# New issue orders for out projection and FFN in a hybrid SSD and latent-attention layer

## The chip, the core and the metric

The kernel runs on one core of a Trainium2 chip. The metric is the device time of one execution in microseconds (us); smaller is better. Five engines of the core take part, each with an instruction stream of its own that it works off in order: TensorE (PE in the profile, with its weight loads listed apart as PEld), VectorE (DVE), ScalarE (ACT), GpSimd (POOL) and SyncE (SP). SP issues most of the transfers. Engines wait for one another through semaphores.

## What is computed

One layer of a streaming encoder for 512 prompt and 64 sample positions, with 1024 channels, in float32. The change lies in the last two parts:

```python
proj = rmsnorm(x, norm_mix) @ w_in
...
x = x + jnp.concatenate([y_ssd, o], axis=-1) @ p['w_out']
hf = rmsnorm(x, p['norm_ffn'])
x = x + (jax.nn.silu(hf @ p['w_gate']) * (hf @ p['w_up'])) @ p['w_down']
...
y = rmsnorm(x, norm_final)
```

`y_ssd` comes from a chunked state-space scan and `o` from latent attention over the same input. `w_gate` and `w_up` are 1024 x 2816, `w_down` is 2816 x 1024.

## The kernel before

**Layout.** Prompt and sample tokens stand side by side, 576 columns, and are worked on in halves of 288 (`TH`), so nearly every matmul is 128x288. Each float32 weight is split into a high part (a cast on ACT, L127) and a low part (a subtraction on DVE, L128), and each product is three matmuls: high by high, high by low, low by high. The names wh_... and wl_... are these two parts.

**Out projection** (L746 to L766). For eight tiles `t` of output channels and both halves, matmuls (L465) collect in a PSUM bank `ps_o`; then DVE adds the bank into `x` (L758). For some tiles ACT copies `x` into the bank first (L462) and the matmuls go onto it.

**FFN.** The gate and up products, and after them the down product, are made by a scheme of seven block products instead of eight. `gu_steps` (L949) shows what matters here:

```python
def m7():
    block_product(z, w, 7)
    act.copy(ur, z)
...
def m4():
    block_product(z, w, 4, onto=True)
    dve.tensor_tensor(ul, z, ul, ALU.add)
```

A product collects in a bank (`ps_x`, `ps_y` or `ps_z`), ACT or DVE reads the bank, and a later product is added onto what is still in it. So the first matmul of product 4 must come after ACT's copy, which must come after the last matmul of product 7: a round trip through PSUM. In `m1` ACT copies ps_x to ps_y (L959), in `m6` and `m7` the bank to `u` (L963, L967); `m2`, `m5`, `m4`, `m3` end in a DVE operation (L971, L975, L979, L983). `down_steps` (L1021) does the same with banks ps_dx, ps_dy and ps_dz; ACT copies go to `db` and `dc` (L1040), from where POOL adds them into `x` by a transfer (L1047), and DVE adds other banks into `x` (L1043, L1063, L1077). The last part of the down product goes through `ps_l` (L1104).

**Weights of the FFN** (`block_weights`, L841). Two SP transfers bring the weights of a block (`gu` or `db`): r2 first (L847), then r1 (L848). DVE makes four block sums: L850 reads r2 alone, L851 to L853 need r1 too. ACT casts part of r2 (`gu_a`, L855), DVE subtracts it for the low part (L861); the other operands go through L127 and L128. So before a matmul can use a low part wl_gu, DVE has made a sum, ACT has cast it and DVE has subtracted.

**What sets the order.** The program is written block by block, and a table then sets the order on each engine. `ISSUE` (L1315) has a text for each of the five engines that lists its instructions, by the numbers they got when they were made, in the order in which they are to be issued; `issue_in_order` (L1274) chains them. `PLACES` (L1286) says which buffer slot each tile gets.

```python
for name, text in ISSUE.items():
    made = [i for i in nc.cur_bb.bb.instructions if i.engine == engines[name].engine]
    order = list(_places(text))
    for a, b in zip(order, order[1:]):
        tc.add_manual_dep(made[b], made[a].name, info, reason="issue order")
```

Of the kernel before, what the change touches and what calls it, by code (L numbers as in the profile page):

```python
# [1328 lines left out]
1190-1192 1227 1193-1198 1291-1297 1199-1201 1228 1202-1204 1286-1288 1215-1217 1207-1210 1218-1220 1211-1214  # L1329
1221-1222 1298 1223 1299 1224 1318 1225-1226 1319 1301-1302 1300 1303-1317 1330-1332 1342-1343 1348-1350 1344-1346  # L1330
1351-1355 1347 1320-1326 1333-1335 1327-1329 1336-1341 1356-1363 1368-1370 1364-1367 1371-1378 1380-1388 1379
1389-1394 1404 1395-1397 1405 1398-1399 1406 1400-1402 1407-1408 1403 1409-1415 1428 1416-1427 1429-1433 1440-1441
1434 1572 1435 1442 1436-1437 1443 1438-1439 1444-1446 1584 1447 1452 1448 1453-1456 1449 1457-1458 1450 1459-1460
1578 1451 1461-1464 1579 1465-1472 1476 1587 1473-1474 1585 1475 1477-1481 1581 1482-1484 1575 1488 1485 1576
1486-1487 1489-1491 1588 1492-1495 1500-1501 1496-1497 1502 1498-1499 1503 1586 1504-1506 1573 1507-1510 1512-1514
1582 1605 1515 1511 1577 1516-1523 1574 1524 1593 1525 1580 1606 1526-1528 1536 1529 1583 1530 1589 1531 1537 1594
1532 1538 1533-1534 1595 1599 1608 1535 1539-1540 1600 1541 1607 1542 1601 1543-1546 1548 1547 1549 1626 1550 1602
1551-1555 1560-1563 1609 1564 1614-1615 1565 1610 1556-1557 1566-1567 1558 1568 1616 1620 1559 1627 1569-1571 1603
1635 1596-1597 1590 1598 1636 1617 1628 1621 1637 1604 1622 1629 1591 1623-1625 1592 1630-1631 1658 1647 1611 1641
1618 1612-1613 1659 1642 1660 1648 1644 1619 1661 1632 1638 1662 1643 1650 1633 1649 1663 1645 1664-1665 1634 1651  # L1340
1666 1656 1639 1653 1640 1652 1667-1668 1646 1669 1654-1655 1657 1694-1695 1670 1682 1671 1696-1697 1672-1675 1698
1676 1683 1699-1700 1677-1678 1718 1701 1679 1702 1719 1684-1685 1720-1721 1680 1703 1681 1686 1722 1704 1723 1687
1724 1688-1689 1725 1705 1690-1691 1706 1692 1707-1709 1693 1710-1711 1726-1728 1730-1732 1729 1733 1712-1716 1754
1734 1778 1717 1779 1735-1736 1755-1756 1780 1737 1757 1766 1738 1742-1744 1739 1745 1740 1758 1746-1747 1767 1748
1781 1741 1782 1759 1749-1750 1783 1751 1760 1752 1768 1761 1784 1769 1785 1770 1786 1753 1787 1771 1762 1772 1763
1802-1803 1788 1773 1789 1774 1804-1813 1764-1765 1775-1777 1862-1863 1838-1839 1864 1840-1841 1865-1866 1842
1867-1868 1843-1844 1869 1845-1848 1790 1870-1871 1814 1849 1791-1792 1872 1793 1873 1815 1794 1874 1795-1796 1816
1875-1876 1850 1877-1878 1797-1798 1817 1879 1818 1799 1819-1820 1880-1881 1821 1800 1882 1822 1801 1851-1855 1883
1823 1884 1824 1856 1826 1886 1827-1829 1825 1857 1830 1858 1831-1832 1859 1887 1885 1833-1835 1888-1889 1860 1890
1836 1861 1891-1893 1837 1894 1898-1900 1895-1897 1901 1910-1911 1902 1912 1946 1913 1903 1914 1904 1922-1924 1934  # L1350
1925-1926 1935 1905-1906 1936 1907 1915 1908 1916-1917 1937 1918-1921 1947-1948 1927 1938 1928 1949 1909 1950 1939
1970 1929-1930 1951 1931 1971 1940-1942 1932 1943 2024 1952 1933 1944 1953 1945 1954 2025 1955 1972 1956 1973 2026
1976 1958-1961 1977 1974 1957 1975 2027 1962-1965 2028 1978 1966-1969 2012 1979 2013 2029 1980-1981 1988 2014 2000
1982-1984 2001 1989-1991 2054 2048 1992 2055-2056 2042 1993 2043 1985-1986 2044 1987 2006 2015-2016 2057 1994 2002
2058 2003-2004 1995 2059 2005 2049 2017 2045 2007 2050 2046-2047 2008-2011 2051 2066 2018-2020 2030 2060 2067
2061-2062 2068 2021 1996 2022 2063-2064 2023 2069 2031-2032 2052 2065 2070 2036 1997 2037 2071-2072 2033 2084 2053
2034 2085 1998 2073 2038 2035 2086 2074-2075 1999 2078 2076 2087 2039-2040 2079-2080 2077 2088-2089 2081 2102 2041
2082 2090-2091 2103 2083 2092-2097 2104-2105 2098 2114 2099 2115 2100 2106 2138 2116-2117 2107-2109 2118 2101 2119
2110-2112 2120 2113 2126 2139 2127-2128 2192 2121 2129-2130 2144-2145 2131 2122 2140 2132-2133 2146-2147 2134-2135
2141 2148 2123-2124 2149 2136-2137 2142 2193 2125 2150 2143 2151 2194 2152 2195-2196 2153 2180 2156 2154 2197  # L1360
2157-2158 2168 2159-2162 2174 2163 2216 2222 2169 2181-2182 2155 2164 2170 2217 2175 2165-2166 2223 2171 2176-2177
# [12 lines left out]
2483-2484 2473 2485-2488 2516 2558 2492-2493 2461 2489 2494 2546 2517 2559 2518 2490 2519 2491 2495-2496 2504 2560
2520-2521 2505 2510 2497 2547 2506 2511 2548 2498-2499 2549 2500 2507 2550 2501 2552 2561 2502 2512 2508 2553 2562
2554 2513 2509 2555 2514-2515 2563 2570 2551 2522-2524 2556 2503 2525 2571 2557 2572 2564 2526 2565-2567 2527 2534
2573 2535 2568-2569 2582 2540 2574 2541 2575 2583 2588 2584 2536-2537 2585 2542-2543 2576 2586 2538-2539 2577 2589
2587 2578 2590 2544 2579-2581 2591 2606-2608 2545 2592 2609 2594 2593 2618 2610 2595 2611 2596-2597 2612 2598
2613-2615 2599 2619-2620 2600 2616 2601-2602 2621 2617 2603-2605 2622-2623 2642 2624-2625 2630-2631 2626 2632 2627
2648-2649 2643 2633 2628 2650 2634 2629 2635-2636 2696 2644 2637 2697 2645 2651-2653 2638-2641 2698-2699 2654-2655  # L1380
2700 2656 2660 2657 2646-2647 2661 2701 2662-2663 2720 2672-2673 2664 2674 2665 2684 2666-2667 2685 2668 2686 2714
2669 2675-2676 2678 2715 2726 2677 2687 2679 2688 2670 2680 2671 2681-2682 2716 2721 2690 2717 2727 2691 2658
2692-2693 2683 2738 2722 2694 2659 2718 2695 2702 2728 2703 2729 2689 2739 2730 2723 2719 2731 2724 2740 2704 2725
2732 2705 2733-2734 2708-2709 2735 2741 2706 2742 2707 2710 2736-2737 2743-2745 2750 2711 2756 2712 2746 2757 2747
2758 2748-2749 2751 2759 2752-2753 2774 2762-2763 2760 2754 2713 2764-2766 2761 2755 2767 2786-2788 2768-2770 2775
2789 2776-2780 2771 2790-2791 2772 2792-2793 2773 2794 2781-2782 2795 2783 2798-2800 2796 2784 2801 2810 2802-2804
2785 2805 2811 2797 2806-2807 2822 2812 2808 2813 2823-2824 2814 2809 2815 2825-2826 2816-2818 2827 2834-2835 2828
# [227 lines left out]
```

## Time and profile before

| what | value |
|---|---|
| time, median of 3 runs | 648.45 us (647.26 to 649.57) |
| profiled execution | 648.09 us, of which 646.0 us are the span |
| mean granted TensorE clock | 0.996 |
| out projection (L465, ps_o) | 159.3 to 257.7 us, with attention at first and FFN products at the end |
| first FFN block | from about 237 us, beside the out projection |
| FFN, gate, up and down | about 268 to 620 us |

A row of the timeline gives start, duration, engine, line, operation and `out<-in` by the program's names, with the shape and a count (x2 is two instructions merged into one row). What stands in brackets is the time that the engine stood idle just before, and who ended it. A row of a window table gives the stretch, its length, then busy time and instructions of PE, PEld, DVE, ACT and POOL, then granted TensorE clock, busy share of the DMA engines and GB/s. A matmul's end is modelled, and consecutive matmuls overlap in the rows; the distance from start to start is the one to read.

### The profile page before, as it was taken

The page shows a single profiled execution, that of the slowest core. Times are in us where ns is not written, and L with a number is a line of the kernel's source. Part 1 is how long each engine was busy: PE and PEld are TensorE (multiplying, and loading weights), DVE is VectorE, ACT ScalarE, POOL GpSimd, SP SyncE. Part 2 cuts the span into 40 slices and gives each one's busy share as a digit, 9 for nine tenths or more (in the row PEclk, how much of TensorE's full clock was granted, in tenths as well). Part 3 has the DMA queues.
Part 4 walks back from the last instruction along what each step waited for, and adds up shares of the span by engine and source line. Part 5 has one row for each costly group of instructions (what it writes and reads, how often), then busy time and mean ns, then how long its engine had stood idle before and what let it go on. Part 6 is the DMA issues. An engine that isn't in the chain of part 4 may idle for free.

```text
span 646.0 us, 11965 instructions
## 1 busy us (share of the span) xinstructions
PE 633.2 (98%) x4639; PEld 601.2 (93%) x4639; DVE 551.6 (85%) x980; ACT 389.6 (60%) x751; POOL 71.3 (11%) x111
## 2 busy tenths in 40 slices
PE   9999999999999999999999999999999999999994
PEld 9799999886787899999999999999999999999994
DVE  6999986899766599999998998789888889997764
ACT  7645425879766479855656565655564656545463
POOL 1422131101000000000012002100210011100022
PEclk9999999999999999999999999999999999999998
DMA  9521183313220221232185238432765166433004
GB/s 316 194 68 60 46 208 137 111 43 132 108 74 33 99 97 66 94 104 73 61 203 147 57 132 203 106 99 99 162 173 118 54 166 159 103 114 131 1 2 146
DMA packets 31560, 72.66 MB, mean 112 GB/s; under 512 B 3706, under 2 KB 11400, under 8 KB 31248
## 3 DMA queue, kind: packets, MB, share of 16 engines
q1 hardware_dynamic: 25360, 60.77, 28.9%
q0 software_dynamic: 5424, 10.57, 9.5%
q8 instruction: 36, 0.59, 0.4%
q10 hardware_dynamic: 720, 0.57, 0.3%
q14 instruction: 20, 0.16, 0.1%
HBM read 58.03 MB, written 3.30 MB: 95 GB/s over the span
## 4 chain that ended last, share of the span: by engine, by line
PE 81%; DVE 11%; DMA 2%; ACT 2%; issue 2%; POOL 0%; POOLq 0%; SPq 0%; DVEq 0%; ACTq 0%
PE ps_x L894 19%; PE ps_z L894 10%; PE ps_dx L1034 8%; PE ps_in L143 8%; PE ps_o L465 7%; PE ps_y L894 5%; PE ps_z L465 4%; PE ps_dz L1034 4%; PE ps_first L143 2%; PE ps_l L1104 2%; PE ps_dy L1034 2%; DMA gu<-in_w_gu 2%; PE sc L680 2%; PE pv L727 2%; PE ptp L702 1%
## 5 line engine op out<-in xcount | busy, mean ns | idle before, releaser
L894 PE MATMUL ps_x<-xop,wh_gu_S 128*128 128x288 f32 x504 | 126.4, 298 | 0.0
L894 PEld LDWEIGHTS ps_x<-xop,wh_gu_S 128*128 128x128 f32 x504 | 87.5, 188 | 1.3 <-DVE u L975 0.3
L894 PE MATMUL ps_x<-xop,wl_gu_S 128*128 128x288 f32 x252 | 73.1, 294 | 0.0
L894 PE MATMUL ps_z<-xop,gu_a 128*128 128x288 f32 x252 | 61.8, 298 | 0.0
L128 DVE TENSOR_TENSOR wl_gu_S<-gu,wh_gu_S 128x1024 fp32r<-128x1024 f32 x44 | 53.5, 1220 | 6.6 <-ACT wh_gu_S L127 6.0
L127 ACT CAST wh_gu_S<-gu 128x1024 fp32r<-128x1024 f32 x44 | 46.1, 1053 | 15.0 <-PE ps_y L894 6.3
L1047 POOL DMA_DIRECT2D x<-db x16 | 14.9, 943 | 296.7 <-ACT db L1040 152.5
L894 PEld LDWEIGHTS ps_x<-xop,wl_gu_S 128*128 128x128 f32 x252 | 47.0, 188 | 0.0
L894 PE MATMUL ps_y<-xop,wh_gu_A 128*128 128x288 f32 x168 | 45.5, 298 | 0.0
L143 PE MATMUL ps_in<-xs,wh_in 128*128 128x288 f32 x256 | 45.5, 298 | 0.0
L894 PEld LDWEIGHTS ps_z<-xop,gu_a 128*128 128x128 f32 x252 | 43.1, 188 | 0.6
L894 PE MATMUL ps_x<-xop,wh_gu_A 128*128 128x288 f32 x168 | 43.1, 297 | 0.0
L894 PE MATMUL ps_z<-xop,wh_gu_S 128*128 128x288 f32 x168 | 43.1, 296 | 0.0
L143 PEld LDWEIGHTS ps_in<-xs,wh_in 128*128 128x128 f32 x256 | 37.8, 189 | 0.2
L127 ACT CAST wh_gu_A<-gu 128x1024 fp32r<-128x1024 f32 x22 | 23.1, 1050 | 16.0 <-PE ps_x L894 6.7
L894 PEld LDWEIGHTS ps_y<-xop,wh_gu_A 128*128 128x128 f32 x168 | 30.2, 188 | 0.4
L894 PEld LDWEIGHTS ps_x<-xop,wh_gu_A 128*128 128x128 f32 x168 | 29.5, 188 | 0.2
L894 PEld LDWEIGHTS ps_z<-xop,wh_gu_S 128*128 128x128 f32 x168 | 29.5, 188 | 0.1
L465 PE MATMUL ps_o<-cat_y,wh_out 128*128 128x288 f32 x128 | 29.0, 313 | 0.5 <-DVE x L758 0.5
L128 DVE TENSOR_TENSOR wl_gu_A<-gu,wh_gu_A 128x1024 fp32r<-128x1024 f32 x22 | 26.8, 1218 | 2.8 <-PE ps_y L894 1.7
L465 PE MATMUL ps_o<-cat_o,wh_out 128*128 128x288 f32 x128 | 27.9, 300 | 0.2 <-DVE x L758 0.2
L143 PE MATMUL ps_in<-xs,wl_in 128*128 128x288 f32 x128 | 27.5, 296 | 0.0
(594 smaller groups left out, 2009.6 us busy)
## 6 DMA issues: line engine op xcount, KB each, us to landing
gu<-in_w_gu SPq DMA_DIRECT2D x44, 512.0 KB, 4.7
db<-in_w_down SPq DMA_DIRECT2D x16, 512.0 KB, 4.5
x<-db POOLq DMA_DIRECT2D x16, 288.0 KB, 4.4
x<-dc POOLq DMA_DIRECT2D x16, 288.0 KB, 4.3
wr_in<-in_w_in SPq DMA_DIRECT2D x8, 512.0 KB, 5.7
wr_out<-in_w_out SPq DMA_DIRECT2D x8, 512.0 KB, 3.2
cumb<-cumD SPq DMA_DIRECT2D x5, 512.0 KB, 4.5
x<-in_xT SPq DMA_DIRECT2D x2, 1152.0 KB, 5.8
```

The lines of the kernel that those rows point to most:

```text
L127: act.copy(hi, raw)
L128: dve.tensor_tensor(lo, raw, hi.bitcast(F32), ALU.subtract)
L143: pe.matmul(ps[:m, hf, :n], w, x[:, hf * n : (hf + 1) * n], start=start and k == 0 and i == 0, stop=stop and k == last and i == 2,)
L465: pe.matmul(ps[:, :n], w, x[:, cols], start=not onto and k == 0 and i == 0, stop=onto or (k == len(terms) - 1 and i == 2), skip_group_chec ...
L680: pe.matmul(s[:, :nk], qs[:, j, q0 : q0 + P], ks[:, j, :nk], start=True, stop=True)
L702: pe.transpose(pp[:, k : k + P], prs[p, i][:, j, b * P : b * P + P], ident)
L727: pe.matmul(pv[64 * j : 64 * j + 64, b * P :], V[b][:, h * HD : (h + 1) * HD], pts[p, b, j], start=b == 0, stop=True, skip_group_check=b > 0,)
L894: pe.matmul(ps, p, q, start=not onto and first and kp == kps[0] and j == 0, stop=onto or (last and kp == kps[-1] and j == 2), skip_group_c ...
L1034: pe.matmul(ps, l, r, start=not onto and k == 0 and j == 0, stop=onto or (k == n - 1 and j == 2), skip_group_check=onto,)
L1047: pool.dma_start(x2[t], v, accum_op=ALU.add)
L1104: pe.matmul(ps, w, x[:, cols], start=first and k == 0 and i == 0, stop=last and k == len(terms) - 1 and i == 2,)
```

## The change

Only rows of `ISSUE` are rewritten, from the out projection on. On PE 2632 matmuls stand at another place than before (moved by -50 to +56 places), on DVE 519 of 980 instructions (-22 to +38), on ACT 324 (-28 to +12), on SP 31 transfers (-2 to +3); POOL's order is the same. The instructions, their operands and the slots in `PLACES` are the same. Of the diff one piece is shown, the tail of SP's row; the others are of this kind:

```diff
     "SP": """
 11-14 16 15 18 17 19-20 22 21 25 24 39 23 37 26 40 33 38 41-43 34 44 32 45 81 46-48 57 64 79 59 58 56 62 61 65 63 60
-83 70 74 67 69 68 71 78 80 88 73 75 72 66 89 77 76 82 86 90-92 87 93 100 103 101-102 104-105 109-113 115 114 116-118
-120 119 121-122 124 123 125-128 130 129 131-132 134 133 135-136 138 137 139-140 142 141 143 145 144 146 148 147 150
-149 151-154 156 155 158 157 159-168 170 169 171-172 175-176 174 177-181
+83 70 74 67 69 68 71 78 80 88 73 75 72 66 89 77 76 82 86 90-92 87 93 100 103 101-102 104-105 109-118 120 119 122-123
+121 124-130 132 131 134 133 136 135 138 137 139-144 146 145 148 147 149-150 152 151 154 153 155-156 158 157 160 159
+161-169 171-172 170 175-176 174 177-181
```

What moves is better seen in the orders themselves, at three places. In the rows, numbers behind a name count the blocks (gu14 is the block of gate and up columns 14) and the buffers; x2 is two instructions in a row.

**PE, FFN block 14, about 488 us.** Product 7 ends with the matmul of xop3 by wl_gu14_S3 into ps_z14; product 4 begins with that of xop0 by gu14_a22. Before:

```order
L894 MATMUL ps_z14_5876<-xop3_3173,wh_gu14_S3_5867 128x288 x2
L894 MATMUL ps_x14_5874<-xop0_2937,wl_gu14_S1_5864 128x288
L894 MATMUL ps_z14_5876<-xop3_3173,wl_gu14_S3_5868 128x288
L894 MATMUL ps_x15_6001<-xop0_2937,wh_gu15_A11_5986 128x288
L894 MATMUL ps_x14_5874<-xop1_3026,wh_gu14_S1_5863 128x288 x2
L894 MATMUL ps_x14_5874<-xop1_3026,wl_gu14_S1_5864 128x288
L894 MATMUL ps_x14_5874<-xop2_3117,wh_gu14_S1_5863 128x288
L894 MATMUL ps_z14_5876<-xop0_2937,gu14_a22_5857 128x288 x2
```

and now:

```order
L894 MATMUL ps_z14_5876<-xop3_3173,wh_gu14_S3_5867 128x288 x2
L894 MATMUL ps_z14_5876<-xop3_3173,wl_gu14_S3_5868 128x288
L894 MATMUL ps_x14_5874<-xop1_3026,wh_gu14_S1_5863 128x288 x2
L894 MATMUL ps_x14_5874<-xop1_3026,wl_gu14_S1_5864 128x288
L894 MATMUL ps_x14_5874<-xop2_3117,wh_gu14_S1_5863 128x288 x2
L894 MATMUL ps_y14_5875<-xop3_3173,wh_gu14_A11_5859 128x288
L894 MATMUL ps_x15_6001<-xop0_2937,wh_gu15_A11_5986 128x288
L894 MATMUL ps_x14_5874<-xop2_3117,wl_gu14_S1_5864 128x288
L894 MATMUL ps_z14_5876<-xop0_2937,gu14_a22_5857 128x288 x3
```

Product 4 starts at the same place of PE's order; the last matmul of product 7 comes three places earlier, so nine places lie between the two starts instead of six.

**DVE, end of the out projection, about 223 to 228 us.** gu0 is the first FFN block, ps_o1_0_0 and ps_o1_0_1 are banks of the out projection that wait to be added into x. Before:

```order
L850 TENSOR_TENSOR gu0_2_2880<-gu0_0_2878 128x512
L852 TENSOR_TENSOR gu0_2_2880<-gu0_2_2880,gu0_1_2879 128x512
L758 TENSOR_TENSOR x2_0_2053<-ps_o1_0_0_2797,x2_0_2053 128x288
L853 TENSOR_TENSOR gu0_3_2881<-gu0_1_2879,gu0_2_2880 128x512
L861 TENSOR_TENSOR gu0_a22_2888<-gu0_0_2878,gu0_a22_2888 128x512
L851 TENSOR_TENSOR gu0_3_2881<-gu0_0_2878,gu0_1_2879 128x512
L758 TENSOR_TENSOR x2_0_2053<-ps_o1_0_1_2811,x2_0_2053 128x288
L128 TENSOR_TENSOR wl_gu0_A11_2891<-gu0_1_2879,wh_gu0_A11_2890 128x1024
```

and now:

```order
L850 TENSOR_TENSOR gu0_2_2880<-gu0_0_2878 128x512
L861 TENSOR_TENSOR gu0_a22_2888<-gu0_0_2878,gu0_a22_2888 128x512
L758 TENSOR_TENSOR x2_0_2053<-ps_o1_0_0_2797,x2_0_2053 128x288
L851 TENSOR_TENSOR gu0_3_2881<-gu0_0_2878,gu0_1_2879 128x512
L852 TENSOR_TENSOR gu0_2_2880<-gu0_2_2880,gu0_1_2879 128x512
L758 TENSOR_TENSOR x2_0_2053<-ps_o1_0_1_2811,x2_0_2053 128x288
L128 TENSOR_TENSOR wl_gu0_A11_2891<-gu0_1_2879,wh_gu0_A11_2890 128x1024
```

gu0_0 is r2, the first transfer, and gu0_1 is r1, the second. The first operation that reads r1 stood ahead of the sum into x of ps_o1_0_0 and now stands behind it; L861, which reads r2 and ACT's cast of it, stands there instead. On ACT that cast (L855, gu0_a22) has moved ahead of the cast of wh_gu0_A11, which reads r1.

**DVE, FFN block 18, about 548 to 552 us.** Before, from the split of S1 to that of S3:

```order
L128 TENSOR_TENSOR wl_gu18_S1_6663<-gu18_2_6648,wh_gu18_S1_6662 128x1024
L850 TENSOR_TENSOR gu19_2_6885<-gu19_0_6883 128x512
L1010 TENSOR_TENSOR pv17_1_6708<-u17_6412,pv17_1_6708 128x288
L852 TENSOR_TENSOR db16_None_2_6775<-db16_None_2_6775,db16_None_1_6774 128x512
L1063 TENSOR_TENSOR x2_1_2055<-ps_dy12_4_6522,x2_1_2055 128x288
L128 TENSOR_TENSOR wl_gu18_S3_6667<-gu18_3_6649,wh_gu18_S3_6666 128x1024
```

and now:

```order
L128 TENSOR_TENSOR wl_gu18_S1_6663<-gu18_2_6648,wh_gu18_S1_6662 128x1024
L852 TENSOR_TENSOR db16_None_2_6775<-db16_None_2_6775,db16_None_1_6774 128x512
L128 TENSOR_TENSOR wl_gu18_S3_6667<-gu18_3_6649,wh_gu18_S3_6666 128x1024
L1077 TENSOR_TENSOR x2_1_2055<-ps_dx12_4_6521,x2_1_2055 128x288
L1063 TENSOR_TENSOR x2_1_2055<-ps_dy12_4_6522,x2_1_2055 128x288
L1077 TENSOR_TENSOR x2_1_2055<-ps_dx12_6_6590,x2_1_2055 128x288
L1010 TENSOR_TENSOR pv17_1_6708<-u17_6412,pv17_1_6708 128x288
```

L850, L1010 and L1063 stood between the two splits; L1063 and L1010 now stand two and four rows behind the second one, L850 farther on.

More of the change, by code (lines that the diff above doesn't have):

```diff
@@ L1333 @@
[L1333 to L1337, printed above, removed]
@@ new lines @@
+1610 1617 1620 1623 1621 1635 1627 1622 1592 1636 1629 1637 1628 1611 1641 1618 1630 1624 1631 1612-1613 1625
+1658-1659 1642 1644 1650 1660 1647 1661-1662 1632-1633 1663 1651 1648 1664-1665 1619 1656 1638-1640 1666 1643 1667
+1634 1668 1645 1669 1646 1649 1652-1654 1657 1694 1670-1672 1695-1697 1673 1682 1698 1655 1674 1699 1675 1700 1718
+1683 1719 1676-1677 1701 1678 1684 1702 1679 1685 1703 1680 1704 1686 1681 1720 1687 1721 1688 1722-1723 1689 1724
+1690-1691 1706 1692-1693 1725 1707 1726 1705 1727-1728 1708-1709 1730 1710-1711 1729 1712 1731-1732 1713-1717
@@ new lines @@
+2484-2485 2460 2486 2461 2487 2492 2517 2493 2560 2518 2546 2504 2494 2488 2519 2552 2495-2497 2553 2505 2520 2547
+2506-2507 2521 2548 2498-2499 2549 2489 2500 2510 2501 2508 2502 2550-2551 2561 2490 2509 2554 2503 2511 2491 2555
+2512-2513 2562-2563 2514-2515 2570 2522-2523 2571 2524 2556 2525 2564 2526-2527 2557 2534-2535 2565 2572 2566-2569
+2540 2582-2584 2573 2541 2574 2542 2585 2575-2576 2536-2539 2588 2577 2589 2586 2578-2579 2590 2543 2580-2581
+2591-2592 2606-2609 2544 2610 2594-2595 2545 2593 2587 2596-2597 2611-2613 2598 2618 2599-2601 2619 2614 2602
@@ new lines @@
+2689 2707 2709 2745 2710 2746-2747 2711 2756 2748 2757 2749 2712 2750 2758 2751 2759-2760 2774 2752-2753 2762-2763
+2754 2775 2764-2765 2713 2766 2776 2761 2777 2786 2778 2755 2787 2767 2788-2790 2768 2791 2769 2779-2780 2792-2793
+2770 2794 2771-2773 2810 2795 2781 2796 2782-2785 2798-2800 2811 2801-2804 2812 2822 2805-2807 2813 2808-2809
+2823-2824 2814-2815 2825 2797 2826 2816-2817 2834-2835 2827-2828 2818-2820 2836 2821 2837 2829 2838-2839 2830 2840
+2858-2859 2846-2847 2870 2841 2860-2861 2871 2842-2844 2862 2848-2850 2863 2831-2832 2851 2845 2852 2864-2865
@@ new lines @@
+3354-3357 3398 3370 3358 3378 3399 3359-3360 3379-3382 3371 3337 3372 3361 3400-3401 3373 3383-3385 3402-3405
+3386-3389 3406 3390-3391 3410 3407 3392-3394 3408-3409 3411 3395-3397 3412-3416 3434 3417 3458 3418 3422 3419
+3423-3424 3435 3425 3420 3426-3428 3459 3446 3429 3436 3447 3430 3460 3431-3433 3437 3448 3438-3439 3421 3440 3449
+3441-3444 3450-3451 3445 3452 3461 3482 3453 3462 3454 3483 3463 3470 3455 3471-3472 3456 3464 3484 3536 3473 3465
+3474 3457 3537 3466 3475-3476 3485 3467 3486 3477 3487 3538 3478 3468 3539 3479 3488 3469 3480 3540 3481 3541 3489
@@ new lines @@
+3524 3490 3525 3491-3493 3512 3526 3494 3500 3554 3501 3495-3496 3513-3514 3497 3502-3503 3555-3556 3515 3504-3505
+3566 3516-3517 3567 3506-3509 3498 3527 3499 3560 3530 3518 3528-3529 3519 3561 3531 3557 3510 3520 3568 3562
+3521-3522 3511 3523 3532 3569 3558 3570 3533-3534 3559 3563-3564 3542 3578 3543 3535 3544 3579 3572 3565 3573
+3545-3546 3574 3580 3575 3581 3576-3577 3582 3547 3590 3583 3591 3548 3571 3584-3585 3592-3593 3549 3586-3588
+3550-3551 3589 3594 3614-3615 3552-3553 3595 3616 3596-3597 3617-3618 3598 3602 3619 3626-3627 3603 3628 3620 3599
@@ new lines @@
+3604-3605 3600-3601 3629 3621 3630 3622-3624 3606 3625 3607 3631 3608 3632 3609-3611 3633 3656 3634 3612-3613 3635
+3657-3660 3636 3661 3650 3638-3643 3651 3637 3644 3704 3645-3649 3652 3662-3663 3705-3706 3653-3654 3664 3668 3665
+3669 3666 3707 3655 3708 3670 3709 3667 3671-3675 3680 3676 3722 3677 3692 3678 3681-3683 3693-3694 3686 3684-3685
+3687-3689 3695 3679 3696 3723 3728 3698 3729 3699 3690 3724 3700 3725 3734-3735 3691 3726 3730 3727 3701-3702
+3736-3737 3703 3731-3732 3746 3733 3740 3710 3747 3711 3738 3741-3742 3716 3739 3758 3712 3759 3743 3697 3717
@@ L1445 @@
+4238 4170 4191 4198 4163 4192 4164 4193 4171-4172 4199 4165 4184 4200 4226 4173 4201 4174-4177 4239 4194 4227
+4207-4208 4228-4230 4240-4242 4202 4243 4231 4185 4209 4195 4262 4210 4186 4232 4211-4212 4263 4233 4213 4234 4214
+4235 4244 4264 4203 4215 4223 4217 4204 4220 4245 4236 4218 4237 4216 4265-4266 4219 4224 4246 4267 4221 4225
+4250-4251 4268-4270 4247 4271 4252 4274 4253 4275 4254 4276-4277 4248 4255 4222 4278-4279 4272 4256 4249 4273
+4257-4259 4280 4260-4261 4281-4391
 """,
@@ L1476 @@
[L1476 to L1478 removed]
+365 336 325 337 321 331 333 366 341 340 338 332 377 334 346 345 342 335 339 344 349 347-348 352 358 343 350-351 368
+353 359-360 356 354 361 355 357 369-373 376 374-375 382 389 378 383-384 379 386 390 385 380 387-388 381 405 397 393
@@ new lines @@
+825 831 834 824 832 860 853 835 842 836 850 859 849 843-844 851 847 845 861 846 838 837 848 852 854 862 839 863 881
+856 866 858 855 857 864-865 868 871 885 877 867 872 878 882 874 880 873 883 876 879 890 886 891 897 889 907 875 884
+888 903 909 887 910 898-899 904 911 900 892 901 919 906 915 908 912 893 914 913 869 905 920-921 923 870 922 917 894
+918 924-925 916 895 928 902 927 937 926 929 896 938 932 931 939 930 933-934 940 935-936 941 946 942 944 943 945 947
+951 949 948 954 950 952-953 955-979
@@ L1504 @@
+621 617-618 622 626 623 620 627-629 632 631 637 633-636 640 638-639 643 645 648 646 651 654 644 649 647 656 641 650
+657 655 659 658 663 660 642 661 664-665 652 666 662 674 667 669 653 675 670 668 677 676 671-672 686 673 684 680 678
+685 682 681 688-690 679 692 687 693-700 691 701-704 683 705-719
 """,
```

256 lines of the change are left out of this document (107 added, 149 removed).

## The prediction

> **What bounds the kernel now.** I read the busy shares and the chain of waits first, then two windows, then the timeline matmul by matmul.
>
> ```profile
> PE 633.2 (98%) x4639; PEld 601.2 (93%) x4639; DVE 551.6 (85%) x980; ACT 389.6 (60%) x751; POOL 71.3 (11%) x111
> PE 81%; DVE 11%; DMA 2%; ACT 2%; issue 2%; POOL 0%; POOLq 0%; SPq 0%; DVEq 0%; ACTq 0%
> 219.00:268.00 49.00, 48.14 (x348) 46.23 (x346) 45.07 (x78) 37.56 (x68) 0.00 (x0) 1.00 0.29 97
> 268.00:620.00 352.00, 350.98 (x2595) 346.71 (x2594) 309.74 (x494) 199.46 (x335) 28.65 (x33) 1.00 0.44 116
> 301.90 0.29 PE L894 MATMUL ps_z<-xop,wh_gu_S 128*128 128x288 f32 x1
> ...
> 303.62 0.29 PE L894 MATMUL ps_z<-xop,wl_gu_S 128*128 128x288 f32 x1
> ```
>
> TensorE is busy for 98% of the span and carries 81% of the chain. The change starts at about 200 us; from 268 to 620 us, the FFN, PE shows 350.98 of 352.00 us. That busy time hides something: a matmul's recorded 0.29 us overlaps the next one's. The pitch tells more. From 301.90 to 303.62 there are 13 intervals, so 0.132 us each. Giving each of the 2595 matmuls the median pitch of its own shape makes 344.3 us, so 7.7 us of the 352.00 is lost between matmuls; from 219 to 268 us the same count loses 3.6. No reordering can win more than these 11.3 us, as no matmul is taken away and the granted clock column already reads 1.00.
>
> Where the 7.7 us goes is seen at single matmuls:
>
> ```profile
> 488.33 0.29 PE L894 MATMUL ps_z<-xop,wl_gu_S 128*128 128x288 f32 x1
> 488.66 0.40 ACT L967 COPY u<-ps_z 128x288 f32<-128x288 f32 x1 [0.93 <-PE ps_z L894]
> ...
> 488.86 0.19 PEld L894 LDWEIGHTS ps_x<-xop,wh_gu_S 128*128 128x128 f32 x1
> ...
> 488.98 0.30 PE L894 MATMUL ps_x<-xop,wh_gu_S 128*128 128x288 f32 x1
> 489.11 0.30 PEld L894 LDWEIGHTS ps_z<-xop,gu_a 128*128 128x128 f32 x2
> 489.11 0.53 PE L894 MATMUL ps_z<-xop,gu_a 128*128 128x288 f32 x2
> 489.35 0.19 PEld L894 LDWEIGHTS ps_x<-xop,wh_gu_S 128*128 128x128 f32 x1
> 489.48 0.29 PE L894 MATMUL ps_x<-xop,wh_gu_S 128*128 128x288 f32 x1
> ```
>
> The matmul at 488.33 is the last of product 7 into ps_z. ACT copies that bank (488.66 to 489.06), and the matmul at 489.11 accumulates onto it. It comes exactly on the pitch (488.98 + 0.13), so it does not wait. Yet its weight load starts with it at 489.11, where an ordinary one starts 0.12 ahead (488.86 for 488.98). The next matmul then starts about 0.235 us later instead of 0.132: two matmuls take 489.11 to 489.48, 0.37 us, where two pitches are 0.26. So an operand that is ready 0.05 us before its use costs 0.10 us although nothing is shown as waiting.
>
> I paired every matmul from 268 to 620 us that waits for a VectorE or ScalarE result with the end of its writer: 334 of them. In 49 the writer ends less than 0.1 us ahead; in 39 by 0.1 to 0.2 (about 0.01 us lost each); in 246 by more, and these lose nothing. The first of the 49 and the last that stands clear in rows:
>
> ```profile
> 273.81 0.40 ACT L967 COPY u<-ps_z 128x288 f32<-128x288 f32 x1
> 274.27 0.65 PE L894 MATMUL ps_z<-xop,gu_a 128*128 128x288 f32 x3
> ...
> 605.49 0.46 DVE L975 TENSOR_TENSOR u<-ps_x,u 128x288 f32<-128x288 f32 x1 [1.55 <-ACT wh_dl L127]
> 606.00 0.52 PE L894 MATMUL ps_x<-xop,wh_gu_S 128*128 128x288 f32 x2
> ```
>
> Together the 49 lose 6.8 us: 2.09 in waits that show and 4.70 in late followers. Of them 37 are round trips through PSUM (matmul, copy or sum, matmul onto it): 0.50 + 3.52 = 4.0 us. Twelve are weight splits that end too late: 1.58 + 1.18 = 2.8 us.
>
> **The change part by part.** No instruction is added or removed; each slot stays. PE moves 2632 of its matmuls, DVE 519, ACT 324, SP 31, POOL none.
>
> *PSUM round trips, -3.6.* The trip of 489.11 needs 489.06 - 488.33 = 0.73 us plus some 0.05 to the next engine, 0.78; the old order gives it 6 places, 6 x 0.132 = 0.79. The new order puts the writer three rows earlier and leaves the user: 9 places, 1.19 us, a margin of 0.4. At 606.00 the distance goes from 6 to 14. Counted over all trips of one kind, the least distance rises from 6 to 9 for the copies of ps_x and ps_z to u, db and dc; to 9 for the sums into u; to 7 to 9 for the rest. Bounds: 0 if ScalarE is late for another reason, 4.0 if every one is cured. ScalarE has room (199.46 busy of 352.00), so I take nine tenths: -3.6.
>
> *Weight splits, -2.2.* The two large ones:
>
> ```profile
> 455.13 1.22 DVE L128 TENSOR_TENSOR wl_gu_A<-gu,wh_gu_A 128x1024 fp32r<-128x1024 f32 x1
> 456.40 0.40 PE L894 MATMUL ps_x<-xop,wl_gu_A 128*128 128x288 f32 x1 [0.43 <-DVE wl_gu_A L128]
> 551.71 1.22 DVE L128 TENSOR_TENSOR wl_gu_S<-gu,wh_gu_S 128x1024 fp32r<-128x1024 f32 x1
> 552.98 0.40 PE L894 MATMUL ps_z<-xop,wl_gu_S 128*128 128x288 f32 x1 [0.59 <-DVE wl_gu_S L128]
> ```
>
> The first loses 0.59 us against its pitch and its follower 0.1; the new order takes a 0.68 us sum (L850) out from ahead of the split and puts the matmul four places later (0.53). The second loses 0.75; its split now comes four VectorE places earlier, three short operations of 0.45 to 0.69 us being moved behind it, and its matmul two places later. Both are cured. The ten small ones hold the other 1.2 us; most get one to three places. From 0 to -2.8; I take -2.2.
>
> *Out projection, -1.2.*
>
> ```profile
> 224.01 0.29 PE L465 MATMUL ps_o<-cat_o,wl_out 128*128 128x288 f32 x1
> ...
> 224.72 0.69 DVE L852 TENSOR_TENSOR gu<-gu,gu 128x512 f32<-128x512 f32 x1 [1.17 <-DMA gu<-in_w_gu]
> 225.33 0.45 DVE L758 TENSOR_TENSOR x<-ps_o,x 128x288 f32<-128x288 f32 x1
> 224.73 1.05 ACT L127 CAST wh_gu_A<-gu 128x1024 fp32r<-128x1024 f32 x1 [4.52 <-DMA gu<-in_w_gu]
> 225.68 0.62 ACT L855 CAST gu_a<-gu 128x512 fp32r<-128x512 f32 x1
> ...
> 225.84 0.54 PE L465 MATMUL ps_o<-cat_y,wh_out 128*128 128x288 f32 x2 [0.48 <-DVE x L758]
> ```
>
> The bank's last matmul ended at 224.30, but its sum stood on VectorE behind L852, which waits for the second weight transfer. PE lost 0.64 us and its follower 0.10. In the new order L861 stands there, which needs the first transfer and ScalarE's cast of it; then x, and only then L851 and L852. ScalarE, idle for 4.52 us up to 224.73, now does that cast ahead of wh_gu_A instead of behind it. So x can run from 224.3, a wait of none: -0.74. The same wait at 238.32 (0.4 with its follower) shrinks by what is moved ahead of it. The losses at 233.39 and 253.33 keep their distances. From -0.5 to -2.0; I take -1.2. Had the cover gone, with x behind another late transfer, it would cost the same 0.64 again.
>
> *New waits, +1.6.* Giving margin to one operand takes it from another, on VectorE above all:
>
> ```profile
> 240.00:260.00 20.00, 19.96 (x148) 19.42 (x147) 19.66 (x36) 18.84 (x38) 0.00 (x0) 1.00 0.23 75
> 280.00:300.00 20.00, 20.00 (x148) 19.55 (x147) 19.87 (x33) 12.03 (x20) 0.00 (x0) 1.00 0.35 103
> 430.00:460.00 30.00, 29.57 (x221) 29.07 (x221) 28.29 (x46) 18.05 (x33) 1.83 (x3) 1.00 0.32 90
> ```
>
> There VectorE has no idle time to give. From 430 on the new order pushes two sums into x (0.45 us each) 38 and 22 places back into this stretch, its splits come one to three places later, and several matmuls come earlier. I count two operands late by up to 0.8 us there, and some six new close pairs elsewhere at 0.10 us plus a little. From 0 to one split each (1.22 + 0.10 = 1.3 us) on five places, 6.6; I take 1.0 + 0.6 = 1.6, near the rows of before, where that stretch lost 1.1 us in all.
>
> *SP's queue.* It issues the same weight loads; 31 move by at most three places. Where a load now stands in front of one whose slot is not free yet, the loads behind it wait. The first VectorE user of a load was mostly 2 to 3 us behind its landing, and the slots come free earlier by the same moves, so zero; one load would come about 1.2 us late, on a VectorE that is idle there. Without that slack it would cost those 1.2 us.
>
> Sum: -3.6 - 2.2 - 1.2 + 1.6 = -5.4. The profiled execution took 648.09 us, 646.0 of it span; it becomes 642.7 with a span of 640.6. Against the median of the runs, 648.45, it is 643.1.
>
> A rule stands against the main term. The Trainium skill, page "TensorE: Matmul & The Clock Gate", in its overview of the engine, says that PE's queue pulls weight loads ahead of matmuls in flight. By it the load behind the late matmul would be done in time, no 0.10 us would hang on a margin, and without the 4.70 us of followers the change would be worth what the first rival below gives. The trace agrees at ordinary matmuls (load at 488.86 for 488.98) but not at 489.11, whose load and whose follower's load (489.35) came late; I go by the rows.
>
> **The rivals.** *Only visible waits go.* If the late follower belongs to any matmul that carries a wait, whatever its margin, the 4.70 us stays. Then 2.09 us and the 1.2 of the out projection, less 1.6 of new waits, make -1.7: 646.8. (The page's rule would give this time too.) Or the waits are eaten further: 648. For it: the profile names no releaser for most of those 0.10 us. Against: 246 matmuls carry such waits with over 0.2 us to spare and keep the pitch. This holds too if the moves cure the places but the time comes back elsewhere.
>
> *Almost all is won.* All three gains at their far ends (4.0 + 2.8 + 2.0) and no new wait: -8.8, 639.7. For it: VectorE has 309.74 of 352.00 in use, so some 42 us of room. Against: that room isn't where it is needed.
>
> *VectorE falls behind.* In the stretches 240 to 330 and 428 to 450 us, where it is 94 to 99% busy, an operation that moves forward delays all splits behind it, with no idle time to catch up in, and PE waits once per split: 1.3 us each. The gains before new waits are 7.0 us, so it decides from six late splits (7.9); with seven, 9.2, the time is 650.7. For it: moves of 38 places into a full queue. Against: before, with the queue just as full, the losses there were 1.1 us from 430 to 460.
>
> **How the numbers follow.** Forecast (-3 to -8) 0.58; almost all 0.10; only visible waits or no net change 0.19; VectorE behind 0.13. The time is the forecast's, 643.1, with a range of its own from 640.5 to 645.5. The range over the cases goes from 640.0, which cuts off part of "almost all", to 648.8, which leaves out VectorE behind. About 0.3%, 1.95 us, is what a measurement of this kernel tells from no change. Faster by more: the forecast, almost all, and a quarter of the third case, 0.73. Within: most of the third, 0.15. Slower: 0.12.
>
> **What would show it.** Right: ACT's copy at what was 488.66 ends 0.3 us or more before its matmul, whose load starts 0.13 ahead and whose follower comes 0.13 later; 268 to 620 shrinks to about 347.5; fewer than 20 close pairs; no wait for x of L758 near 225. Wrong: PE waits for wl splits from 240 to 330 or 428 to 460 of over 3 us; or the close pairs are gone and the time is not, which would refute the 0.10 us.

## The result: 639.6 us, 8.7 us less

The changed kernel took 639.63 us (median of 4 runs, 639.24 to 640.2), the kernel before 648.32 beside it; the ratio is 0.9866 with an interval from 0.9847 to 0.9885. Four later series on other occasions gave 641.36, 639.72, 639.92 and 639.6 us, which is 6.4, 8.0, 7.8 and 8.2 us less than the kernel before beside them. The forecast was 643.1 us with a range from 640.0 to 648.8: the direction was right, and the gain was larger than the range allowed.

The page's first rows and its chain are read first; the profile of the changed kernel has

```profile
span 637.5 us, 11950 instructions
PE 626.2 (98%) x4639; PEld 598.0 (94%) x4639; DVE 551.4 (86%) x980; ACT 390.4 (61%) x751; POOL 70.7 (11%) x111
PE 48%; issue 1%; DVE 1%; ACT 1%; POOL 1%; POOLq 0%; DVEq 0%
```

PE is still busy for 98% of the span, so this share tells nothing of the gain: it counts the overlapping 0.29 us of each matmul, late followers included. The chain's shares add up to only about half of the span here, so its 48% cannot be held against the 81% before. What does tell is how long a like piece of the program takes. The windows of the kernel before, from the same place of PE's order (the 1695th matmul) to the last gate or up matmul:

```profile
270.45:610.70 340.25, 339.23 (x2514) 335.07 (x2512) 303.37 (x482) 193.60 (x326) 27.77 (x32) 1.00 0.45 120
```

and of the changed kernel, from one matmul farther on:

```profile
268.13:601.43 333.30, 333.20 (x2508) 332.26 (x2507) 303.30 (x483) 194.16 (x329) 27.75 (x32) 1.00 0.46 121
```

From the same matmul, which starts at 268.00 now, the FFN takes 6.8 us less with the same work on VectorE and ScalarE (303 and 194 us). Four matmuls, 0.6 us, have only moved behind the window's end; the rest, some 6 us, was lost time. By the count used in the prediction (each matmul at the median pitch of its shape) the FFN lost 7.66 us before and 1.93 now. That count hangs on the median: a tenth of a nanosecond in it makes 0.25 us over some 2500 matmuls, so half a microsecond between two profiles means nothing. Instead of 49 close pairs between 268 and 620 us there are 7.

The matmul of the prediction's example, which stood at 489.11:

```profile
481.94 0.29 PE L894 MATMUL ps_z<-xop,wl_gu_S 128*128 128x288 f32 x1
...
482.27 0.40 ACT L967 COPY u<-ps_z 128x288 f32<-128x288 f32 x1 [0.77 <-PE ps_z L894]
...
482.99 0.45 PEld L894 LDWEIGHTS ps_z<-xop,gu_a 128*128 128x128 f32 x3
...
483.12 0.56 PE L894 MATMUL ps_z<-xop,gu_a 128*128 128x288 f32 x3
483.38 0.32 PEld L894 LDWEIGHTS ps_x<-xop,wh_gu_S 128*128 128x128 f32 x2
483.51 0.43 PE L894 MATMUL ps_x<-xop,wh_gu_S 128*128 128x288 f32 x2
```

The trip takes what it took (481.94 to 482.67), but the user comes at 483.12, 0.45 us behind. Its weight load starts 0.13 us ahead, and three matmuls take 483.12 to 483.51, 0.39 us, the bare pitch.

The wait for x at 225.84 is gone too, as the rows of VectorE and PE show:

```profile
223.47 0.69 DVE L861 TENSOR_TENSOR gu_a<-gu,gu_a 128x512 fp32r<-128x512 f32 x1
224.08 0.45 DVE L758 TENSOR_TENSOR x<-ps_o,x 128x288 f32<-128x288 f32 x1
224.45 0.68 DVE L851 TENSOR_TENSOR gu<-gu,gu 128x512 f32<-128x512 f32 x1
224.87 0.43 PE L465 MATMUL ps_o<-cat_y,wh_out 128*128 128x288 f32 x2
```

In the stretch from the 1282nd matmul to the 1695th (out projection and first FFN block) 60.61 us became 58.02 in this profile. It is not always so: the four later profiles of the changed kernel show 59.2, 59.6, 58.0 and 59.3, and the experiments tell why.

### The profile page after: what moved, and what is told of

Read it like the earlier page. It is cut to its first block, busy times and chain, and to the rows that moved or that the text cites. A ratio compares the mean times of both kernels' runs of the same rounds, so it can differ in the third digit from the quotient of the medians.

```text
span 637.5 us, 11950 instructions
## 1 busy us (share of the span) xinstructions
PE 626.2 (98%) x4639; PEld 598.0 (94%) x4639; DVE 551.4 (86%) x980; ACT 390.4 (61%) x751; POOL 70.7 (11%) x111
## 4 chain that ended last, share of the span: by engine, by line
PE 48%; issue 1%; DVE 1%; ACT 1%; POOL 1%; POOLq 0%; DVEq 0%
PE ps_x L894 17%; PE ps_dx L1034 9%; PE ps_z L894 9%; PE ps_dz L1034 5%; PE ps_y L894 4%; PE ps_dy L1034 2%; PE ps_l L1104 2%; POOL x L1157 0%; DVE x L1145 0%; DVE sq_last L1194 0%; DVE ss L1192 0%; POOL ss L1238 0%; POOLq L1600 0%; ACT sq L1233 0%; ACT x L1149 0%
```

## The experiments

All kernels compute the same; only the order tables differ. Each edit is shown in short: what is taken from the old and the new tables, or the rows of one of the places that are moved. In the tables' words, "old" and "new" are the orders before and after the change.

### Which part of the program the gain comes from

At about 270 us old and new orders of each engine hold the same instructions ahead of a cut (1694 on PE, 456 on DVE, 343 on ACT, 78 on SP), so they can be joined there.

```diff
 e1_out
-PE, DVE, ACT, SP: old ahead of the cut, old behind
+PE, DVE, ACT, SP: new ahead of the cut, old behind
 e2_ffn
-PE, DVE, ACT, SP: old ahead of the cut, old behind
+PE, DVE, ACT, SP: old ahead of the cut, new behind
```

> New orders up to about 270 us on every engine, old orders behind. Margin theory: the losses between matmuls up to there fall by 2.3 us and the FFN keeps its close pairs, so about 646.0 us. If the stages depend on each other (the out projection's gain is only kept because the FFN's new order takes it up), less than 1 us is won.

> Old orders up to about 270 us, new orders behind. Margin theory: the FFN wins its 6.2 us by itself, about 642.1 us, and this and the other half add up to the whole gain of 8.7. If the FFN's gain needs the earlier start of transfers and sums in the out projection, clearly less than 6.

The new FFN behind the old out projection took 642.0 us against 648.12, ratio 0.9909 (0.9891 to 0.9927): 6.1 us less, as expected. The new out projection alone took 647.32, ratio 0.999 (0.998 to 1.0): of the 2.3 us that were expected hardly 0.8 are left. In its profile the stretch up to 270 us is shortened as expected (58.43 us), but the FFN behind it loses 9.04 us instead of 7.66. Some 0.6 us of that is lost at 268 to 274 us, by operands that are late now that PE comes 2 us earlier, and 0.8 us at one matmul (476.98), whose operand stands on VectorE behind a weight transfer that took 8.4 us instead of 7.6. VectorE and PE there:

```profile
474.30 0.69 DVE L850 TENSOR_TENSOR gu<-gu 128x512 f32<-128x512 f32 x1 [3.28 <-DMA gu<-in_w_gu]
...
476.98 0.40 PE L894 MATMUL ps_x<-xop,wh_gu_A 128*128 128x288 f32 x1 [0.63 <-DVE g L983]
```

So the second theory, that the out projection's gain is only kept because the FFN's new order leaves room for it, fits this profile, but it is not shown by the times: the series of the changed kernel that followed (e5_after) gained 6.4 us, no more than the two halves together.

In e2_ffn one wait is left that is worth a look. ACT, then PE:

```profile
350.57 0.40 ACT L963 COPY u<-ps_x 128x288 f32<-128x288 f32 x1 [3.74 <-DMA x<-db]
...
351.02 0.40 PE L894 MATMUL ps_x<-xop,wh_gu_S 128*128 128x288 f32 x1 [1.71 <-ACT u L963]
```

The copy writes a buffer that GpSimd's transfer of db into x still reads. It waits for a landing, and PE for the copy. The same pair is the one old close pair that the changed kernel did not open (347.68 in its profile, margin 0.05 us); its wait was 0 to 0.4 us in the five profiles of the changed kernel.

### Whether a margin is worth time

e4_open leaves all orders as they were and only brings matmuls of other banks ahead of the user of each close trip through PSUM. At the example:

```diff
 L894 MATMUL ps_x14_5874<-xop2_3117,wh_gu14_S1_5863 128x288
-L894 MATMUL ps_z14_5876<-xop0_2937,gu14_a22_5857 128x288 x2
 L894 MATMUL ps_x14_5874<-xop2_3117,wh_gu14_S1_5863 128x288
 L894 MATMUL ps_y14_5875<-xop3_3173,wl_gu14_A11_5860 128x288
+L894 MATMUL ps_z14_5876<-xop0_2937,gu14_a22_5857 128x288 x2
 L894 MATMUL ps_x14_5874<-xop2_3117,wl_gu14_S1_5864 128x288
```

> The old orders of all engines but PE; on PE two or three unrelated matmuls are brought ahead of the first matmul behind each of 35 of the 36 close round trips through PSUM in the FFN (162 places hold another matmul). Visible waits removed: 0.44 us; late followers removed: 3.31 us. Margin theory: 3.7 us less, about 644.6 us. Rival that only visible waits cost time: 0.4 us less, 647.9. Rival that the new orders win by what VectorE, ScalarE and the transfers do earlier: no change.

It took 645.41 us, ratio 0.9958 (0.9946 to 0.9971), 2.7 us less (3.0 in the span of the profile). The 0.4 us of visible waits cannot be that. What is missing to 3.7 went in part where PE now comes sooner to a split that is no sooner done. VectorE, then PE:

```profile
548.84 1.22 DVE L128 TENSOR_TENSOR wl_gu_S<-gu,wh_gu_S 128x1024 fp32r<-128x1024 f32 x1
...
550.11 0.40 PE L894 MATMUL ps_z<-xop,wl_gu_S 128*128 128x288 f32 x1 [0.82 <-DVE wl_gu_S L128]
```

This is the wait of 552.98, 0.75 us before and 0.98 now. A dozen places that lost nothing before lose 0.05 to 0.15 us each, while the wait of 456.40 shrinks from 0.59 to 0.19. In the whole FFN the close pairs fell from 48 to 23 and the loss from 7.66 to 4.57 us.

The opposite test takes margin away from the changed kernel: in each of 35 trips the first matmul behind the copy or sum goes two, three or four places forward, past matmuls of other banks. Three places, at the example:

```diff
 L894 MATMUL ps_x14_5874<-xop2_3117,wh_gu14_S1_5863 128x288 x2
+L894 MATMUL ps_z14_5876<-xop0_2937,gu14_a22_5857 128x288
 L894 MATMUL ps_y14_5875<-xop3_3173,wh_gu14_A11_5859 128x288
 L894 MATMUL ps_x15_6001<-xop0_2937,wh_gu15_A11_5986 128x288
 L894 MATMUL ps_x14_5874<-xop2_3117,wl_gu14_S1_5864 128x288
-L894 MATMUL ps_z14_5876<-xop0_2937,gu14_a22_5857 128x288 x3
+L894 MATMUL ps_z14_5876<-xop0_2937,gu14_a22_5857 128x288 x2
```

> The changed kernel again, as the base for the three that follow: 639.6 us.

> The changed kernel, with the first matmul behind each of 35 round trips through PSUM (margins 0.45 to 0.51 us) two places earlier on PE, so margins of 0.19 to 0.24. In both traces a follower is late by 0.155 us less the margin. Margin theory by that: no loss, 639.6 us. Rival that a margin under some 0.4 us costs something: 1 us or more.

> The same 35 matmuls three places earlier: margins of 0.06 to 0.11 us, so still no visible wait. Margin theory: 35 followers late by 0.155 less the margin, 2.8 us more, 642.4 us. Rival that only visible waits cost time: no change, 639.6.

> The same 35 matmuls four places earlier: the operand would be late by 0.07 to 0.13 us. Margin theory: wait and follower together 7.4 us more, 647.0 us. Rival that only visible waits cost time: the waits alone, 3.8 us more, 643.4.

| kernel | margin of the 35 | median us | FFN lost us | more than the base: measured, expected |
|---|---|---|---|---|
| e5_after | 0.45 to 0.51 | 641.36 | 1.90 | |
| e6_less2 | 0.19 to 0.24 | 641.05 | 1.42 | -0.3, 0 |
| e7_less3 | 0.06 to 0.11 | 644.13 | 4.47 | 2.8, 2.8 |
| e8_less4 | would be -0.08 to -0.02 | 647.44 | 8.72 | 6.1, 7.4 |

Ratios to the kernel before: 0.9894 (0.9866 to 0.9922), 0.9939 (0.9916 to 0.9962) and 0.9991 (0.9981 to 1.0). Moving 35 matmuls by four places each gives back nearly the whole change: 6.1 us, and 6.8 in the FFN of the traces, where the visible waits alone would cost 3.8. Three places, which add no visible wait, cost 2.8 us. That difference is not clear of the spread by the times alone, as the five runs of the base lie between 640.49 and 644.72 us; what carries it is the trace, where the FFN loses 2.6 us more, in followers late by 0.05 to 0.12 us each. The example with three places less:

```profile
484.24 0.40 ACT L967 COPY u<-ps_z 128x288 f32<-128x288 f32 x1 [0.77 <-PE ps_z L894]
...
484.43 0.43 PE L894 MATMUL ps_x<-xop,wh_gu_S 128*128 128x288 f32 x2
484.69 0.19 PEld L894 LDWEIGHTS ps_z<-xop,gu_a 128*128 128x128 f32 x1
484.69 0.39 PE L894 MATMUL ps_z<-xop,gu_a 128*128 128x288 f32 x1
...
484.92 0.29 PE L894 MATMUL ps_y<-xop,wh_gu_A 128*128 128x288 f32 x1
```

The user comes on its pitch (484.56 + 0.13), no wait is shown, the load is not ahead, and the next matmul follows after 0.23 us. With two places less:

```profile
482.01 0.40 ACT L967 COPY u<-ps_z 128x288 f32<-128x288 f32 x1 [0.77 <-PE ps_z L894]
...
482.47 0.19 PEld L894 LDWEIGHTS ps_z<-xop,gu_a 128*128 128x128 f32 x1
...
482.60 0.29 PE L894 MATMUL ps_z<-xop,gu_a 128*128 128x288 f32 x1
...
482.73 0.29 PE L894 MATMUL ps_x<-xop,wh_gu_A 128*128 128x288 f32 x1
```

A margin of 0.19 us is as good as one of 0.45: the load starts 0.13 us ahead, the follower comes after 0.13.

### The out projection: a wait that wanders

e3_swap takes the new order of eight VectorE places and one ScalarE pair at 223 to 228 us into the old kernel, those that the section on the change shows and the places of wl_gu0_A11, wl_out1_2 and L853 behind them:

```diff
 DVE, from the first sum behind L850 to the sum of ps_o1_1_0
-L852 gu, L758 x, L853 gu, L861 gu_a, L851 gu, L758 x, L128 wl_gu, L128 wl_out
+L861 gu_a, L758 x, L851 gu, L852 gu, L758 x, L128 wl_gu, L128 wl_out, L853 gu
 ACT
-L127 wh_gu, L855 gu_a
+L855 gu_a, L127 wh_gu
```

> The old orders, with eight VectorE places and one ScalarE pair at 223 to 228 us taken from the new ones. Margin theory: the wait of 0.64 us at 225.84 and its follower's 0.10 go, 0.7 us in all, about 647.6 us. Rival: the sums that were moved are late at the next bank and the time comes back there, 648.3.

A miss on both sides: 649.42 us, ratio 1.0024 (1.0014 to 1.0033), 1.3 us more than before. The wait at 225.84 is gone, but L853 is now behind two splits, and what follows is a chain over both engines:

```profile
229.14 0.69 DVE L853 TENSOR_TENSOR gu<-gu,gu 128x512 f32<-128x512 f32 x1
...
229.86 1.05 ACT L127 CAST wh_gu_S<-gu 128x1024 fp32r<-128x1024 f32 x1 [1.88 <-DVE gu L853]
...
231.73 1.04 ACT L127 CAST wh_out<-wr_out 128x1024 fp32r<-128x1024 f32 x1
...
232.80 1.23 DVE L128 TENSOR_TENSOR wl_out<-wr_out,wh_out 128x1024 fp32r<-128x1024 f32 x1 [1.47 <-ACT wh_out L127]
233.94 0.45 DVE L758 TENSOR_TENSOR x<-ps_o,x 128x288 f32<-128x288 f32 x1
...
234.45 0.66 PE L465 MATMUL ps_o<-cat_o,wh_out 128*128 128x288 f32 x3 [1.55 <-DVE x L758]
```

ScalarE's cast waits for L853, a cast of wh_out stands behind it, the split of wl_out waits for that, and x behind the split: PE loses 1.71 us there.

e10_dveact gives VectorE and ScalarE their whole new orders up to the cut, with PE's old one:

```diff
-DVE, ACT: old ahead of the cut, old behind; PE, SP: old
+DVE, ACT: new ahead of the cut, old behind; PE, SP: old
```

> The new orders of VectorE and ScalarE up to about 270 us; PE, SP and all that follows as before. If the out projection's gain is made by what those two engines do earlier, PE follows and 1.5 to 2.3 us are won by 270 us, some of it lost again in the FFN: 647.0 us. If it needs PE's new places too, no gain or a loss: 648.1 or more.

651.04 us, ratio 1.0053 (1.004 to 1.0065): 3.3 us more. Without PE's new places the new orders of the two others lose time. PE's new places alone were not run, and neither was such a mix in the FFN.

The three profiles of the changed kernel with a longer first stretch lose most of it at one matmul. The rows of SP, VectorE and PE in one of them (e9_after):

```profile
219.48 0.33 SPq L848 DMA_DIRECT2D gu<-in_w_gu  x1
...
225.80 0.69 DVE L851 TENSOR_TENSOR gu<-gu,gu 128x512 f32<-128x512 f32 x1 [1.52 <-DMA gu<-in_w_gu]
226.41 0.69 DVE L852 TENSOR_TENSOR gu<-gu,gu 128x512 f32<-128x512 f32 x1
227.01 0.45 DVE L758 TENSOR_TENSOR x<-ps_o,x 128x288 f32<-128x288 f32 x1
...
227.52 0.40 PE L465 MATMUL ps_o<-cat_y,wh_out 128*128 128x288 f32 x1 [0.86 <-DVE x L758]
```

The second sum into x stands behind L851 and L852, and these behind the second transfer of gu. In the first profile that transfer was issued at 219.70 and landed after 4.6 us; here it took 6.3. Over the five profiles it took 4.6, 5.9, 6.3, 4.6 and 6.0 us, and the time lost at this matmul was 0, 0.62, 1.02, 0 and 0.76 us.

e13_banks and e15_banks put sums into x ahead of the operations that need this transfer or follow from it; PE first uses what those make at 243 us (three sums in e13, a fourth in e15):

```diff
 DVE of the changed kernel, behind L861 gu_a (x by number of the sum)
-x1, L851, L852, x2, wl_gu, wl_out, L853, x3, wl_gu, wl_gu, x4, wl_out, xop, xv, x5
+e13: x1, x2, L851, L852, L853, wl_out, x3, wl_gu, wl_gu, x4, wl_gu, wl_out, xop, xv, x5
+e15: x1, x2, L851, L852, L853, wl_out, x3, wl_gu, wl_gu, x4, wl_gu, x5, xop, xv, xv, wl_out
```

> The changed kernel, as the base on this chip: 639.6 to 641.4 us.

> The changed kernel, with eleven VectorE places at 224 to 232 us in another order: the sums of three banks into x ahead of the block sums and splits that need the second transfer of gu, whose first use on PE is at 243 us. If the wait at 227 us (0 to 1.1 us from one profile to another) is the transfer's landing, it goes for good: 0.5 to 1.3 us less than the changed kernel in the median. If only places on VectorE count, the same time.

> The changed kernel, as the base on this chip: 639.6 to 641.4 us.

> As e13_banks, and the next sum into x (the one that made PE wait 1.29 us at 234.95 there) also ahead of the split and the four operations that stood before it. If those waits only wandered along VectorE's queue, they are gone now, as the operations passed over have their first use at 237 us and later: 1.2 us less than e13_banks and 0.3 to 1.3 less than the changed kernel on the same chip. If VectorE is simply full up to 270 us, the wait appears at the next sum and the time stays.

e13 took 640.19 us beside 639.92 for the changed kernel, e15 641.42 beside 639.6 (all four runs of e15 above all four of its base). Neither is less than its base, so both forecasts of a gain missed. In e13 the wait at 227 us is gone, although the transfer landed at 225.1 there, after 5.9 us, as in the profile that lost 0.62; but 1.29 us are lost at x5 (234.95). In e15 that is gone as well, and ScalarE waits for an xv:

```profile
236.89 1.25 ACT L826 CAST xop<-xv 128x576 fp32r<-128x576 f32 x2 [1.94 <-DVE xv L821]
...
237.62 0.40 PE L894 MATMUL ps_p<-xop,wh_gu_S 128*128 128x288 f32 x1 [1.23 <-ACT xop L826]
```

So the first theory of e13 (the landing) is right about the wait, and the second of e15 about its cure. VectorE is full in this stretch; the window of the changed kernel has it busy for 43.79 of 44.00 us:

```profile
224.00:268.00 44.00, 44.00 (x324) 43.14 (x323) 43.79 (x76) 38.45 (x66) 0.00 (x0) 1.00 0.28 92
```

What is taken from one operand is missing at the next.

### A wider margin for the rest

e11_wider opens the changed kernel's remaining close pairs in the manner of e4_open, on PE alone:

```diff
-U, F1, F2
+F1, F2, U          (U: one of 15 users with a close operand; F: 2 to 6 matmuls of other banks)
```

> The changed kernel once more, as the base on this chip: between 639.6 and 641.4 us, the two medians so far.

> The changed kernel, with 2 to 6 unrelated matmuls brought ahead of 15 matmuls whose operand still comes just in time (93 PE places). In the trace of the changed kernel those cost 1.05 us in waits and 1.28 in late followers, and two more waits come and go with a transfer's landing (up to 0.6 and 0.3 us). Margin theory: 1.5 to 2.3 us less than the changed kernel on the same chip. Rival that the last close pairs are set by VectorE or a transfer: the waits stay with one place more, 0.5 us less or none.

641.31 us beside 639.72 for the changed kernel, ratio to before 0.9896 (0.9881 to 0.9911): no gain, if anything a loss, so the theory missed. The profile shows that a copy to dc waits for a landing, as the copy in e2_ffn does, and that the copy to db stands behind it; the two cost 2.0 us:

```profile
342.64 0.40 ACT L1040 COPY dc<-ps_dz 128x288 f32<-128x288 f32 x1 [2.59 <-DMA x<-dc]
...
343.09 0.41 PE L1034 MATMUL ps_dz<-pb1y,db_a 128*128 128x288 f32 x1 [1.26 <-ACT dc L1040]
...
344.33 0.41 PE L1034 MATMUL ps_dx<-pb1o,wh_db_S 128*128 128x288 f32 x1 [0.44 <-ACT db L1040]
```

And four new close pairs stand at 304 to 311 us, where VectorE is full. Whether the late landing comes from these moves or by chance stays open with one profile. No version beats the changed kernel.

## Why the prediction was wrong: the mechanism held, the sizes did not

Every gain in the sum was put too small and the new waits too large, and so the time fell 0.4 us below the range. The largest errors are the new waits (0.65 us), the out projection (0.6 in the mean of five profiles, 1.4 in the first) and the weight splits (0.6). Of the five series of the changed kernel one, 641.36 us, lies inside the range; the other four lie 0.1 to 0.4 below it.

**The price of a close operand: right.** 0.10 us for an operand that ends 0.05 us ahead, none from 0.2 us on, was the main term, and e6, e7 and e8 give it a dose and a response. The rival that only visible waits count would have e7 at the base's time and e8 3.8 us above it; it is refuted by the rows of e7 and by e8, whose FFN loses 6.8 us more. The rule that the prediction weighed is from the Trainium skill, page "TensorE: Matmul & The Clock Gate", in its overview table: by it PE's queue pulls weight loads ahead of matmuls in flight. The traces agree at 482.47 in e6, but not at 484.69 in e7, where the operand is close; that every such load is done in time, as the prediction read the rule, does not hold here, and the measurement decides.

**PSUM trips, -3.6: mechanism right, too small by 0.3.** Of the 37, 36 have 0.28 us or more now, worth 3.85 of the 4.0. The discount of a tenth stood for ScalarE being late elsewhere, which happened once (347.68).

**Weight splits, -2.2: too small by 0.6.** All twelve were cured, 2.76 us; the smallest margin among them is 0.31. The split of 552.98 now has 1.42.

**Margins from 0.1 to 0.2: left out.** The prediction put about 0.01 us on each of these 39 and no term in the sum. They cost 0.57 us, and 6 with 0.11 are left: 0.46 us won.

**New waits, +1.6: too large by 0.65.** This is the step that failed most: 1.0 us was put on two operands that were to be late from 430 to 460 us, and 0.6 on six new close pairs elsewhere. In the FFN the new close pairs cost 0.95 us, all from 282 to 309 us but one of 0.08. From 430 to 460 us, where two operands were to be late by up to 0.8 us, nothing at all is lost. The window of that piece of the program in the changed kernel, to be held against the one at 430 in the prediction:

```profile
425.40:455.00 29.60, 29.60 (x226) 29.60 (x225) 27.46 (x45) 18.55 (x33) 1.72 (x2) 1.00 0.34 107
```

VectorE has 2.1 us of 29.6 free. The likely reason, which no run tests, is that places were counted by which a split is pushed back, without all that is taken out ahead of it. "VectorE falls behind" did not come about there; e3 and e10 show that its mechanism is real in the out projection.

The four FFN terms, as they came out, are -3.85 - 2.76 - 0.46 + 0.95 = -6.1 where the prediction had -3.6 - 2.2 + 1.6 = -4.2. The profiles' loss falls by 5.7 us in the first and by 6.1 in the mean of five (from 7.66 to 1.58).

**Out projection, -1.2: too small, and not made up as foreseen.** The stretch up to 270 us is 58.81 us in the mean of five profiles, 1.8 less than before, and between 1.0 and 2.6 less in single ones. The 0.74 us at 225.84 goes in all five, as foreseen, and so does the whole 0.42 at 238.32, which was only to shrink. The loss at 253.33 (0.31) was to stay and goes too, with 0.36 at 243.71 and 249.46. Against that, the next sum into x stands behind the same transfer: in the three profiles where it lands late, this costs 0.62 to 1.02 us and some 0.5 behind it. The prediction had named that case, at 0.64, but had put nothing on it in the sum. What it did not see is that the eight places alone lose time (e3), and that the new orders of VectorE and ScalarE lose time without PE's new places (e10). In the first profile the transfer landed early; that part of the gain of 8.7 us is luck.

**SP's queue, 0: right.** In the profile of the changed kernel no wait on PE in the FFN goes back to a weight load; the one transfer that holds something up there is GpSimd's (347.68).

The case that came closest was "almost all is won", at 639.7 us. The prediction gave it a chance of 0.10 and ended the range ahead of it, at 640.0. That its number is so near is partly luck. In the FFN it had 4.0 + 2.8 and no new wait where 3.85 + 2.76 + 0.46 - 0.95 came; it had 2.0 for the out projection where 1.0 to 2.6 came. The room on VectorE, spoken against there, sufficed in the FFN.

## What to carry to other kernels

On an engine that is busy 98% by its records, compare the starts with the bare pitch: operands that arrive just in time show no wait and can still cost the follower a large part of a pitch. Leave about 0.2 us, here two matmuls, between an operand's end and its use; the 0.45 us of the changed kernel were worth no more than the 0.19 of e6. Moving one operation hardly removes a wait on an engine without idle time: in e3, e13 and e15 it went to a later operand in the queue, so such orders are to be judged over the whole stretch, and on several profiles where a transfer's landing is part of it.

## What the runs showed of the hardware

The lateness of a follower depends on the margin without a step. From the rows of both kernels between 268 and 615 us, every matmul that waits for VectorE or ScalarE, by how long before its start the writer ended:

```
margin us       matmuls   next matmul late by, us (mean)
under 0.06          30    0.104
0.06 to 0.08        18    0.091
0.08 to 0.10         6    0.073
0.10 to 0.12         6    0.053
0.12 to 0.14         9    0.026
0.14 to 0.16        11    0.013
0.16 to 0.20        19    0.00
over 0.20          567    0.00
```

That is 0.155 us less the margin, about the time that a weight load of such a pair starts ahead plus some 0.02; the last is only how the numbers lie, no run tests it. Landing times were the other surprise: two profiles of one program had 4.6 and 6.3 us for the same 512 KB transfer.
